# A causal convolution over eight taps: half of one more output pair moved from VectorE to ScalarE and GpSimd, later output buffers, tap 0 in four parts, and new instruction orders

## The chip, the cores and the metric

The kernel runs on one core of one Trainium2 chip. The time is the device time of one execution in microseconds. A core has TensorE (PE, the matrix engine; its weight loads are shown apart as PEld), VectorE (DVE), ScalarE (ACT), GpSimd (POOL) and SyncE (SP), each with an instruction queue of its own that is worked off in order. Transfers are issued from the queues of SP, POOL and ACT.

## The reference

`x` is (8, 4096, 512) and `kernel` (8, 512, 512), both f32; the output has the form of `x`.

```python
for k in range(K):                      # K = 8 taps
    shifted = x if k == 0 else concatenate([zeros(B, k, D), x[:, :-k, :]], axis=1)
    out += matmul(shifted, kernel[k])
```

Row t of the output is the sum over k of x[t - k] times kernel[k].

## The kernel before

The 8 x 4096 time steps are laid out as 128 partitions of 256 steps each, so that one matmul handles the same step of 128 stretches. The first 4 steps (HEAD) are computed tap by tap (`direct`). The other 252 are 21 blocks of 12 steps. A block is four *nodes*, PL, MI, H1 and H0, numbered k = 1 to 84 (node 4m + 1 is PL of block m). A node makes a part of a convolution out of sums and differences of rows of x and of taps, so that fewer products are needed than in the direct way; two nodes of block 0, k = 3 and 4 (LEAF), go with fewer sums and more products.

A *product* is four matmuls of 128x128 by 128x512 in bf16. A node has 9 of them (a leaf 11), named in the orders below as a1, a0, u, v0, v1, l00, l01, l10, l11. The other steps of a node are:

- DVE: `z` (differences or sums of rows of x, seven rows, XR to Z), `A`, `s` (sums of rows of Z, to S), `F0` and `F1` (sums of rows of S), all bf16 with both inputs in SBUF; `d0` and `d1` (PSUM and the f32 tile DT, to PSUM); `e0` and `e1` (a pair of PSUM banks and an output tile, to an output tile `y`).
- ACT: the copy after a1, the seeds `s0` and `s1` (they start the PSUM pairs of v0 and v1), `dt` (fills DT), the copies of PL's pairs to `cc`, and E0 (the half of an H1 pair).
- POOL: loads of later rows of x (`r0` to `r2`), the halves ga0, gb0, ga1 and gb1 of the middle output rows (cc and dd), and ya0, the second half of H1's first pair.
- SP: the stores and the transposes of x into XR (`x12` to `x20`).

In the order a token is a step and a node counted from the block's PL: `F0.2` is F0 of H1 (0 PL, 1 MI, 2 H1, 3 H0, then 4 PL and 5 MI of the next block), so `z.5` is the z of the next block's MI. DVE works about one node ahead of the products that use its sums. The output tiles come from a pool of five buffers of 128x1024 f32 (`ypool`); a block takes six (cc0, cc1, dd0, dd1, yy0, yy1), so a tile waits for a store of an older one. PSUM has four pairs of banks: pp0 to pp2 are taken in turn by the two pairs of each node, pp3 is the first accumulator of each node.

What sets the order is written by hand: a list of calls for the start, and then the string ORDER, once a block. Within an engine instructions run in just that order. `behind` makes a POOL instruction wait for the latest DVE sum that stands ahead of it in the list.

At the start x and the taps are loaded; tap 0 in one load, the others as loads of 512 KB. Weight sums (`wsum`, `plus`, lines L84 of DVE with 128x2048) prepare the nodes' weights, the first four rows are transposed on PE, and `fill` keeps PE working with matmuls of zeros.

Of the kernel before, what the change touches and what calls it, by code (L numbers as in the profile page):

```python
# [14 lines left out]
def kernel(  # L15
# [244 lines left out]
    def node_e(n, b_):  # L260
        p, t = n.p[b_], n.t + 2 * b_
        first = n.k <= 4
        if n.a == PL:
            cc[b_] = y_tile()
            if first:
                nc.scalar.mul(out=cc[b_], in_=p, mul=0.5)
            else:
# [2 lines left out]
                nc.scalar.mul(out=dd[b_], in_=cc[b_], mul=-0.5)  # L270
        elif n.a == MI:
            if first:
                dd[b_] = y_tile()
                stt(dd[b_], p, -0.5, cc[b_], ADD)
            else:
                stt(dd[b_], p, 0.5, dd[b_], ADD)
        elif n.a == H1:
            yy[b_] = yy.get(b_) or y_tile()
            if first or b_ == HI:
                tt(yy[b_], p, dd[b_], ADD if first else SUB)  # L280
                store(t, yy.pop(b_))
            else:
                tt(yy[b_][:, 0], p[:, 0], dd[b_][:, 0], SUB)
        elif n.k == len(nodes) - 1 and b_ == HI:
            for j, eng in ((HI, nc.scalar), (LO, nc.sync)):
                stt(dd[b_][:, j], dd[b_][:, j], -1.0, p[:, j], SUB)
                eng.dma_start(out=orr[:, t + 8 + j, :], in_=dd[b_][:, j])
        else:
            if first:
                tt(dd[b_], dd[b_], p, SUB)  # L290
            else:
                stt(dd[b_], dd[b_], -1.0, p, SUB)
# [2 lines left out]
    def node_E(n):
        if n.a == H1 and n.k > 4:
            yy[LO] = yy.get(LO) or y_tile()
            nc.scalar.copy(out=yy[LO][:, 1], in_=n.p[LO][:, 1])

    def node_y(n):  # L300
        if n.a == H1 and n.k > 4:
            y = yy.pop(LO)
            behind(nc.gpsimd.tensor_tensor(out=y[:, 1], in0=y[:, 1], in1=dd[LO][:, 1], op=SUB))
            store(n.t, y)
# [4 lines left out]

    def middle_half(n, b_, j):  # L310
        behind(nc.gpsimd.tensor_tensor(out=cc[b_][:, j], in0=cc[b_][:, j], in1=dd[b_][:, j], op=ADD), b_ > j and n.k)  # L311
# [143 lines left out]
    fill(pair(3))
    fill(pair(3))
    here(nc.scalar.copy, 0, "x0", 0, 2)
    transpose_pe("h4", 3, H, 4, 8)
    here(nc.scalar.copy, 0, "x0", 2, 4)
    fill(pair(2))  # L460
    history(nc.scalar.copy, -4, "h4")
    direct(0, 1)
    go(3, "v0")
    go(2, "d1")
    direct(0, 0)
    direct(0, 2)
    direct(0, 3)
    direct(4, 2)
    fill(pair(2))
    load_w(1)  # L470
    direct(4, 0)
    direct(1, 1)
    direct(1, 3)
    wsum(MI, HI, HI)
    load_w(5)
    load_w(3)
    wsum(MI, HI, LO)
# [25 lines left out]
    go(4, "F1")
    direct(7, 3)
    wsum(MI, LO, LO)
    history(nc.scalar.copy, -7, "h3")
    direct(6, 3)
    wsum(H0, MID, HI)
    plus((LO, HI))
    direct(3, 2)  # L510
    direct(6, 2)
    direct(5, 2)
    direct(5, 0)
    direct(2, 1)
    wsum(MI, LO, HI)
    transpose_pe("x4", 3, xin[4], 0, 4)
    wsum(PL, MID, HI)
    transpose_pe("x8", 2, xin[8], 0, 2)
    direct(7, 0)
    here(nc.scalar.copy, 4, "x4", 0, 2)  # L520
    wsum(MI, LO, MID)
    wsum(PL, LO, MID)
    wsum(MI, MID, HI)
# [179 lines left out]
```

## Time and profile before

| | us |
|---|---|
| three runs | 717.39, 718.18, 718.66 (median 718.18) |
| span of the profiled execution, first to last instruction | 717.2 |
| PE busy | 696.0 (97%) |
| DVE busy | 683.3 (95%) |
| ACT busy | 287.7 (40%) |
| POOL busy | 167.5 (23%) |

The profile is one execution; the page gives its span, and no other time of its own. The three runs are whole executions, and their median stands 1.0 us above the span. The page groups instructions by line, engine and tile. "Idle before" is the engine's time without work ahead of them, and the releaser is what ended it. The timeline lists one engine's instructions in order with start and duration; the chain of waits follows what ended last backwards; the windows give each engine's busy time within a stretch.

### The profile page before, as it was taken

The numbers are of one execution on the slowest core, as the hardware profiler recorded it, in microseconds if no ns is written. First come the engines' busy times: TensorE is split into PE (matmuls) and PEld (weight loads), VectorE is DVE, ScalarE is ACT, GpSimd is POOL, SyncE is SP. The second block draws the span as 40 slices with busy tenths as digits, with TensorE's granted clock in tenths as the row PEclk, the third lists the DMA queues.
The fourth block names the chain that finished last, engine by engine and source line by source line (L and its number), as shares of the span: only waits on it lengthen the run. The fifth ranks groups of instructions, "written<-read, shape, count | busy, mean of one in ns | idle before, by whom it ended". The sixth has DMA issues, their size and how long they took to land.

```text
span 717.2 us, 8960 instructions
## 1 busy us (share of the span) xinstructions
PE 696.0 (97%) x3205; PEld 315.0 (44%) x3270; DVE 683.3 (95%) x767; ACT 287.7 (40%) x448; POOL 167.5 (23%) x180
## 2 busy tenths in 40 slices
PE   7989999999999999999999999999999999999995
PEld 3444444444444444444444444444444444444442
DVE  1899999999999999999999999999999999999994
ACT  3043244343435444343443434353443434444341
POOL 4200012213131221304122131312213041221212
PEclk9999999999999999999999999999999999999999
DMA  9996988788797878879788887977788698855414
GB/s 194 209 225 139 235 156 243 158 233 181 206 226 174 233 167 231 181 189 217 182 241 158 231 184 205 229 176 229 168 237 174 189 224 178 238 119 186 157 68 175
DMA packets 159515, 138.86 MB, mean 194 GB/s; under 512 B 130160, under 2 KB 134256, under 8 KB 159344
## 3 DMA queue, kind: packets, MB, share of 16 engines
q1 hardware_dynamic: 145312, 99.37, 46.6%
q0 software_dynamic: 13728, 38.15, 31.6%
q10 hardware_dynamic: 432, 0.79, 0.3%
q8 instruction: 25, 0.41, 0.2%
q14 instruction: 18, 0.15, 0.1%
HBM read 77.33 MB, written 99.09 MB: 246 GB/s over the span
## 4 chain that ended last, share of the span: by engine, by line
PE 84%; DVE 5%; issue 5%; DMA 0%; POOL 0%; DVEq 0%; POOLq 0%
PE pp L127 84%; DVE w L84 2%; DVE Z L84 2%; DVE y L87 1%; DVE S L84 1%; DMA out_dram<-y 0%; POOL y L311 0%; DVE y L84 0%; DVE F L84 0%; DVE pp L87 0%; DVE pp L84 0%; POOL xd L93 0%; DVEq L84 0%; DVEq L87 0%; POOLq L93 0%
## 5 line engine op out<-in xcount | busy, mean ns | idle before, releaser
L127 PE MATMUL pp<-w,F 128*128 128x512 bf16 x1285 | 310.4, 379 | 3.2 <-DVE pp L87 1.3
L127 PE MATMUL pp<-w,Z 128*128 128x512 bf16 x941 | 231.9, 379 | 2.7 <-DVE Z L84 1.7
L127 PEld LDWEIGHTS <-F 128*128 128x128 bf16 x1312 | 128.3, 98 | 157.6 <-issue 3.4
L311 POOL TENSOR_TENSOR y<-y 128x512 f32<-128x512 f32 x80 | 101.7, 1272 | 406.0 <-DVE F L84 266.1
L127 PE MATMUL pp<-w,S 128*128 128x512 bf16 x658 | 157.5, 379 | 0.7
L84 DVE TENSOR_TENSOR Z<-XR 128x2048 bf16<-128x2048 bf16 (+3 forms) x109 | 154.5, 1435 | 2.5
L127 PEld LDWEIGHTS <-Z 128*128 128x128 bf16 x960 | 92.3, 98 | 118.2 <-DVE Z L84 9.4
L198 ACT COPY pp<-pp 128x512 f32<-128x512 f32 x82 | 46.7, 570 | 221.1 <-PE pp L127 221.1
L84 DVE TENSOR_TENSOR S<-Z 128x2560 bf16<-128x2560 bf16 (+1 forms) x81 | 114.5, 1413 | 0.0
L84 DVE TENSOR_TENSOR F<-S 128x1024 bf16<-128x1024 bf16 x160 | 111.1, 694 | 1.9 <-PE pp L127 1.9
L127 PEld LDWEIGHTS <-S 128*128 128x128 bf16 x672 | 65.8, 98 | 79.4 <-issue 0.2
L214 ACT COPY pp<-pp 128x512 f32<-128x512 f32 (+1 forms) x84 | 48.9, 582 | 76.5 <-PE pp L127 76.5
L93 POOL DMA_DIRECT2D xd<-in_x_dram x61 | 32.7, 536 | 103.7 <-DVE F L84 48.6
L84 DVE TENSOR_TENSOR pp<-DT,pp 128x512 f32<-128x512 f32 x82 | 56.3, 687 | 0.2 <-PE pp L127 0.2
L87 DVE SCALAR_TENSOR_TENSOR pp<-pp,DT 128x512 f32<-128x512 f32 x82 | 56.5, 689 | 0.0
L216 ACT ACTIVATE pp<-pp 128x512 f32<-128x512 f32 (+1 forms) x84 | 50.1, 596 | 15.2 <-PE pp L127 9.8
L84 DVE TENSOR_TENSOR Z<-Z 128x1024 bf16<-128x1024 bf16 x78 | 53.4, 684 | 0.7
L87 DVE SCALAR_TENSOR_TENSOR y<-pp,y 128x1024 f32<-128x1024 f32 x42 | 51.0, 1215 | 0.0
L220 ACT COPY DT<-pp 128x512 f32<-128x512 f32 x82 | 48.9, 597 | 2.6 <-PE pp L127 2.6
L268 ACT COPY y<-pp 128x1024 f32<-128x1024 f32 x40 | 40.6, 1016 | 22.9 <-PE pp L127 21.7
L87 DVE SCALAR_TENSOR_TENSOR y<-y,pp 128x1024 f32<-128x1024 f32 (+1 forms) x41 | 48.3, 1181 | 0.3 <-PE pp L127 0.3
L270 ACT ACTIVATE y<-y 128x1024 f32<-128x1024 f32 x40 | 42.3, 1057 | 2.8 <-DMA out_dram<-y 0.6
(35 smaller groups left out, 248.5 us busy)
## 6 DMA issues: line engine op xcount, KB each, us to landing
out_dram<-y SPq DMA_DIRECT2D x126, 512.0 KB, 4.2
xd<-in_x_dram POOLq DMA_DIRECT2D x61, 512.0 KB, 5.6
w<-in_kernel_dram POOLq DMA_DIRECT2D x8, 512.0 KB, 16.8
w<-in_x_dram SPq DMA_DIRECT2D x1, 1024.0 KB, 4.8
w<-in_x_dram POOLq DMA_DIRECT2D x2, 512.0 KB, 14.0
XR<-xd SPq DMA_TRANSPOSE x61, 4.8
out_dram<-y ACTq DMA_DIRECT2D x3, 256.0 KB, 3.4
w<-in_x_dram POOLq DMA_DIRECT2D x2, 256.0 KB, 18.1
```

The costliest lines, as they stand in the source:

```text
L84: last["dve"] = nc.vector.tensor_tensor(out=o, in0=a, in1=b, op=op)
L87: last["dve"] = nc.vector.scalar_tensor_tensor(out=o, in0=a, scalar=by, in1=b, op0=MUL, op1=op)
L93: return nc.gpsimd.dma_start(out=o, in_=src)
L127: nc.tensor.matmul(bank, lhsT=comp[:, c * P:(c + 1) * P], rhs=w[:, c, :], start=start and c == 0, stop=c == DC - 1, skip_group_check=True)
L198: nc.scalar.copy(out=n.q[:, 0], in_=n.q[:, 1])
L214: nc.scalar.copy(out=o, in_=q)
L216: nc.scalar.mul(out=o, in_=q, mul=-1.0)
L220: nc.scalar.copy(out=DT, in_=n.q[:, 0])
L268: nc.scalar.copy(out=cc[b_], in_=p)
L270: nc.scalar.mul(out=dd[b_], in_=cc[b_], mul=-0.5)
L311: behind(nc.gpsimd.tensor_tensor(out=cc[b_][:, j], in0=cc[b_][:, j], in1=dd[b_][:, j], op=ADD), b_ > j and n.k)
```

## The change

**H1's second pair.** `SPLIT = (0, 1)`: for both pairs of H1 DVE now adds only the first half. The other half is copied by ACT (E1) and completed by POOL (ya1).

**Output buffers and algebra.** `cc` is written as 0.5 p (before: p) and doubled by ACT later (m0, m1) instead of a -0.5 copy to `dd`; `dd` is now made by DVE at MI, one node later, in a fresh buffer. H0's last operation becomes a plain subtraction. In block 0 the middle rows are made by POOL in halves, not by DVE (g0, g1).

**S of H1 and F.** H1's `s` is written with its five rows in reverse, H0's at rows 1 to 4; F sums adjacent rows then, without the repeated or strided operands of before.

**The start.** Tap 0 is loaded as four transfers and multiplied in four column parts, 22 early filler matmuls instead of 14, the cast of the first rows is split otherwise, a copy goes to DVE, and the order of sums, loads and transposes is new.

**The orders.** ORDER and the list at the start (SETUP) are new throughout.

```diff
-LEAF, EARLY = (3, 4), 6
+LEAF, EARLY, SPLIT = (3, 4), 6, (0, 1)
...
+            self.rev = a == H1 and not self.leaf
...
         if n.shares:
-            tt(n.s[:, 0:4], n.z[:, n.o + 1:n.o + 5], n.z[:, n.o + 3:n.o + 7], ADD)
...
+            tt(n.s[:, 1:5], z[:, o + 1:o + 5], z[:, o + 3:o + 7], ADD)
+        elif n.rev:
+            tt(n.s[:, ::-1], z[:, o:o + 5], z[:, o + 2:o + 7], ADD)
...
+        i = 2 - a if n.rev and not n.whole else a
+        tt(F[:, a:b], n.s[:, i:i + b - a], n.s[:, i + 1:i + 1 + b - a], ADD)
...
         if n.a == PL:
             cc[b_] = y_tile()
-            if first:
-                nc.scalar.mul(out=cc[b_], in_=p, mul=0.5)
-            else:
-                nc.scalar.copy(out=cc[b_], in_=p)
-                dd[b_] = y_tile()
-                nc.scalar.mul(out=dd[b_], in_=cc[b_], mul=-0.5)
+            nc.scalar.mul(out=cc[b_], in_=p, mul=0.5)
         elif n.a == MI:
-            if first:
-                dd[b_] = y_tile()
-                stt(dd[b_], p, -0.5, cc[b_], ADD)
-            else:
-                stt(dd[b_], p, 0.5, dd[b_], ADD)
+            dd[b_] = y_tile()
+            stt(dd[b_], p, -0.5, cc[b_], ADD)
         elif n.a == H1:
             yy[b_] = yy.get(b_) or y_tile()
-            if first or b_ == HI:
-                tt(yy[b_], p, dd[b_], ADD if first else SUB)
+            if b_ in SPLIT:
+                tt(yy[b_][:, 0], p[:, 0], dd[b_][:, 0], ADD)
+            else:
+                tt(yy[b_], p, dd[b_], ADD)
                 store(t, yy.pop(b_))
...
+    def node_E(n, b_):
+        yy[b_] = yy.get(b_) or y_tile()
+        nc.scalar.copy(out=yy[b_][:, 1], in_=n.p[b_][:, 1])
+
+    def node_y(n, b_):
+        y = yy.pop(b_)
+        behind(nc.gpsimd.tensor_tensor(out=y[:, 1], in0=y[:, 1], in1=dd[b_][:, 1], op=ADD))
+        store(n.t + 2 * b_, y)
+
+    def twice(n, b_):
+        nc.scalar.mul(out=cc[b_], in_=cc[b_], mul=2.0)
...
+    def direct_part(c):
+        w = W[(K - 1) >> 2, (K - 1) >> 1 & 1, (K - 1) & 1]
+        for t in range(HEAD):
+            nc.tensor.matmul(pd[t // 2][:, t % 2], lhsT=XR[:, place(t), c * P:(c + 1) * P], rhs=w[:, c, :],
+                             start=c == 0, stop=c == DC - 1, skip_group_check=True)
...
     ORDER = """
...
-        d1.3 e0.3 u.4 l11.3 z.5 s0.4 F0.4 A.5 s1.4 dt.4 ga1.2 v0.4 v1.4 l10.3 d0.4 a1.5 d1.4 l00.4 l01.4
+        E1.2 u.4 dt.4 gb1.2 s0.4 l11.3 l10.3 e0.3 v0.4 z.5 ya1.2 s1.4 F0.4 v1.4 A.5 ga1.2 a1.5 d0.4 d1.4
```

**What moves: DVE and POOL in a block.** DVE around the second half of a block, from H0's d0 to the next PL's d0; `y<-pp,y` is H1's second output pair, `y<-y,pp` H0's first. Before:

```order
L84 TENSOR_TENSOR pp_1348<-DT,pp_1348 128x512
L84 TENSOR_TENSOR y<-pp_1277,y 128x1024
L84 TENSOR_TENSOR S<-Z 128x2560
L87 SCALAR_TENSOR_TENSOR pp_1345<-pp_1345,DT 128x512
L87 SCALAR_TENSOR_TENSOR y<-y,pp_1348 128x1024
L84 TENSOR_TENSOR Z<-XR 128x1536
L84 TENSOR_TENSOR Z<-XR 128x2048
L84 TENSOR_TENSOR F<-S 128x1024
L84 TENSOR_TENSOR Z<-Z 128x1024
L84 TENSOR_TENSOR pp_1400<-DT,pp_1400 128x512
```

Now:

```order
L84 TENSOR_TENSOR pp_1356<-DT,pp_1356 128x512
L87 SCALAR_TENSOR_TENSOR pp_1358<-pp_1358,DT 128x512
L84 TENSOR_TENSOR S<-Z 128x2560
L84 TENSOR_TENSOR y<-pp_1302,y 128x512
L84 TENSOR_TENSOR y<-y,pp_1356 128x1024
L84 TENSOR_TENSOR Z<-XR 128x1536
L84 TENSOR_TENSOR Z<-XR 128x2048
L84 TENSOR_TENSOR F<-S 128x1024
L84 TENSOR_TENSOR Z<-Z 128x1024
L84 TENSOR_TENSOR pp_1414<-DT,pp_1414 128x512
```

H1's second add shrinks to 128x512 and stands behind d1 of H0 and S of the next PL. POOL in the same block, with the buffers' numbers and what each row waits for. Before (L303 is ya0, L311 the middle halves):

```order
L311 TENSOR_TENSOR y_1205<-y_1205,y_1207 128x512 [waits DVE_49]
L93 DMA xd_1338<-in_x_dram 128x2048 [waits DMASW6_49,DVE_49]
L303 TENSOR_TENSOR y_1328<-y_1328,y_1207 128x512 [waits DMAHW4_49,DVE_49,DMAHW6_49,Activation_49,Pool_49]
L93 DMA xd_1360<-in_x_dram 128x2048 [waits DMASW7_49]
L311 TENSOR_TENSOR y_1270<-y_1270,y_1272 128x512 [waits DMAHW4_49,DMAHW0_49,DVE_49]
L311 TENSOR_TENSOR y_1270<-y_1270,y_1272 128x512 [waits DVE_49]
```

Now (L293 is ya0 and ya1, L300 the middle halves):

```order
L300 TENSOR_TENSOR y_1227<-y_1227,y_1279 128x512 [waits DVE_49]
L93 DMA xd_1373<-in_x_dram 128x2048 [waits DMASW1_49,DVE_49]
L293 TENSOR_TENSOR y_1348<-y_1348,y_1279 128x512 [waits DMAHW6_49,DMAHW4_49,Activation_49]
L93 DMA xd_1395<-in_x_dram 128x2048 [waits DMASW2_49,DVE_49]
L300 TENSOR_TENSOR y_1268<-y_1268,y_1330 128x512 [waits DMAHW3_49,DVE_49,Activation_49]
L293 TENSOR_TENSOR y_1405<-y_1405,y_1330 128x512 [waits DMAHW2_49,DVE_49,Activation_49]
L300 TENSOR_TENSOR y_1268<-y_1268,y_1330 128x512 [waits DVE_49]
```

The new add ya1 (y_1405) stands between the two middle halves gb1 and ga1, behind DVE's z of the next block's MI.

**ACT ahead of H0's seeds.** From the copy after H0's a1 to its dt. Before (L298 is E0, L216 and L214 the seeds):

```order
L198 COPY pp_1298<-pp_1298 128x512
L298 COPY y<-pp_1274 128x512
L216 ACTIVATE pp_1345<-pp_1298 128x512
L214 COPY pp_1348<-pp_1298 128x512
L220 COPY DT<-pp_1298 128x512
```

Now (L289 is E0, L297 m1, L218 and L220 the seeds, L224 dt):

```order
L202 COPY pp_1318<-pp_1318 128x512
L289 COPY y<-pp_1304 128x512
L297 ACTIVATE y<-y 128x1024
L218 COPY pp_1356<-pp_1318 128x512
L220 ACTIVATE pp_1358<-pp_1318 128x512
L224 COPY DT<-pp_1318 128x512
```

The doubling of cc1 stands between E0 and the first seed, and the two seeds change places.

**DVE at the start, up to the first node's A.** Weight tiles have numbers (w_71 is tap 7's); w_97 holds the first node's A and S. Before:

```order
L84 TENSOR_TENSOR w_96<-w_96 128x2048
L84 TENSOR_TENSOR w_89<-w_87,w_88 128x2048
L84 TENSOR_TENSOR w_96<-w_96 128x2048
L84 TENSOR_TENSOR w_94<-w_91,w_88 128x2048
L84 TENSOR_TENSOR w_96<-w_96 128x2048
L84 TENSOR_TENSOR Z<-XR 128x2560
L84 TENSOR_TENSOR w_97<-Z 128x1024
L84 TENSOR_TENSOR w_97<-Z 128x1536
L84 TENSOR_TENSOR Z<-XR 128x1024
L84 TENSOR_TENSOR w_78<-w_75,w_72 128x2048
```

Now:

```order
L84 TENSOR_TENSOR w_85<-w_83,w_81 128x2048
L84 TENSOR_TENSOR w_96<-w_96 128x2048 x2
L84 TENSOR_TENSOR Z<-XR 128x2560
L84 TENSOR_TENSOR Z<-XR 128x1024
L84 TENSOR_TENSOR w_97<-Z 128x1024
L84 TENSOR_TENSOR w_97<-Z 128x1536
L84 TENSOR_TENSOR w_97<-Z 128x1024
L84 TENSOR_TENSOR w_93<-w_90,w_87 128x2048
```

Of the rows before, the sums w_89, w_94 and w_93 come behind the first node's A and S, w_78 ahead of its z; the second part of z (128x1024) comes ahead of A.

More of the change, by code (lines that the diff above doesn't have):

```diff
@@ L287, in node_e @@
                 eng.dma_start(out=orr[:, t + 8 + j, :], in_=dd[b_][:, j])
         else:
[L289 to L292, printed above, removed]
+            tt(dd[b_], dd[b_], p, SUB)
             store(t + 8, dd[b_])
[L295 to L304, printed above, removed]
@@ L306, in middle @@
-    def middle(n, b_):
-        stt(cc[b_], cc[b_], 2.0, dd[b_], SUB)
-        store(n.t + 4 + 2 * b_, cc[b_])
+    def node_E(n, b_):
[7 more added lines that the diff above has]
+        nc.scalar.mul(out=cc[b_], in_=cc[b_], mul=2.0)
     def middle_half(n, b_, j):
-        behind(nc.gpsimd.tensor_tensor(out=cc[b_][:, j], in0=cc[b_][:, j], in1=dd[b_][:, j], op=ADD), b_ > j and n.k)
+        behind(nc.gpsimd.tensor_tensor(out=cc[b_][:, j], in0=cc[b_][:, j], in1=dd[b_][:, j], op=SUB), b_ > j and n.k)
@@ L455 @@
[L455 to L477, printed above, removed]
@@ L503 @@
[L503 to L523, printed above, removed]
@@ new lines, with act @@
+    """.split()
+    def act(token):
+        name, _, k = token.partition(".")
+        if token in FIRST:
+            FIRST[token]()
+        elif k:
+            if name in PARTS:
+                done.add((name[0], int(k)))
+                PARTS[name](nodes[int(k)])
+            else:
+                do(name, int(k))
+        elif name.startswith("out"):
+            direct_out(int(name[3:]))
+        elif name[0] == "f":
+            fill(pair(int(name[1:])))
+        elif name[0] == "w":
+            load_w(int(name[1:]))
+        elif name[0] == "T":
+            transpose_x(int(name[1:]))
+        elif name[0] == "L":
+            load_x(int(name[1:]))
+        elif name[0] == "B":
+            behind(load_x(int(name[1:])))
+        elif name[0] == "t":
+            p = PE_T[name[1:]]
+            transpose_pe(name[1:], *p)
+        elif name[0] == "q":
+            n, c = K - 1, int(name[1:])
+            load(W[n >> 2, n >> 1 & 1, n & 1][:, c:c + 1], kr[:, c:c + 1, 0, :])
+        elif name[0] == "P":
+            direct_part(int(name[1:]))
+        elif name[0] in "cv":
+            t, h = int(name[2:3]), name[3:]
+            lo = 0 if h == "a" else 2
+            src = "x" + str(t)
+            here(nc.scalar.copy if name[0] == "c" else nc.vector.tensor_copy, {0: 0, 4: 4, 8: 8, 9: 10}[t], src, lo, lo + 2)
+        elif name[0] == "D":
+            direct(int(name[1]), int(name[2]))
+        elif name[0] in "sp":
+            a, b_, c_ = (int(i) for i in name[1:])
+            if name[0] == "p":
+                plus((b_, c_))
+            else:
+                wsum(a, b_, c_)
```

254 lines of the change are left out of this document (55 added, 199 removed).

## The prediction

> **What bounds the kernel now.** I read the page first, then the waits, the chain of waits, the middle of the run by windows and by groups, and last the timelines of VectorE (DVE), GpSimd (POOL) and TensorE (PE) at the start, in one block and at the end. The page, and under it the middle by windows (columns: us, then busy us of PE, weight loads, DVE, ACT, POOL, clock, DMA):
>
> ```profile
> PE 696.0 (97%) x3205; PEld 315.0 (44%) x3270; DVE 683.3 (95%) x767; ACT 287.7 (40%) x448; POOL 167.5 (23%) x180
> PE pp L127 84%; DVE w L84 2%; DVE Z L84 2%; DVE y L87 1%; DVE S L84 1%; DMA out_dram<-y 0%; POOL y L311 0%; DVE y L84 0%; DVE F L84 0%; DVE pp L87 0%; DVE pp L84 0%; POOL xd L93 0%; DVEq L84 0%; DVEq L87 0%; POOLq L93 0%
> ...
> 310.00:550.00 240.00, 238.84 (x1090) 107.98 (x1110) 238.02 (x273) 102.32 (x164) 59.70 (x61) 1.00 0.81 200
> ```
>
> PE carries 84% of the chain, but in the middle DVE is busy 238.02 of 240.00 us: both are full, at clock 1.00. The chain gives PE's pace and shows the one place in the middle where it leaves PE:
>
> ```profile
> 282.52 10.74 PE pp L127 x49
> 293.26 0.05 issue
> 293.32 7.52 PE pp L127 x34
> ...
> 303.11 1.21 DVE y L87
> ...
> 307.52 9.02 PE pp L127 x41
> ```
>
> A piece repeats every 10.74 + 0.05 = 10.79 us. It lists 49 matmuls, but 1110 weight loads in 240.00 us make 0.216 us each, so 50 matmuls stand in 10.79 (one record is missing): 0.2158 us per matmul. A block has 4 nodes of 36, 144 matmuls = 31.08 us. The DVE timeline (start, us) shows one block of the same engine from Z to Z:
>
> ```profile
> 319.47 1.21 DVE L84 TENSOR_TENSOR Z<-XR 128x2048 bf16<-128x2048 bf16 x1
> ...
> 332.27 1.48 DVE L84 TENSOR_TENSOR S<-Z 128x2560 bf16<-128x2560 bf16 x1
> 333.67 0.69 DVE L87 SCALAR_TENSOR_TENSOR pp<-pp,DT 128x512 f32<-128x512 f32 x1
> 334.27 1.21 DVE L87 SCALAR_TENSOR_TENSOR y<-y,pp 128x1024 f32<-128x1024 f32 x1
> 335.40 2.08 DVE L84 TENSOR_TENSOR Z<-XR 128x1536 bf16<-128x1536 bf16 x2
> 337.40 0.68 DVE L84 TENSOR_TENSOR F<-S 128x1024 bf16<-128x1024 bf16 x1
> 338.00 0.68 DVE L84 TENSOR_TENSOR Z<-Z 128x1024 bf16<-128x1024 bf16 x1
> 338.61 0.68 DVE L84 TENSOR_TENSOR pp<-DT,pp 128x512 f32<-128x512 f32 x1
> ...
> 339.81 0.78 DVE L84 TENSOR_TENSOR F<-S 128x1024 bf16<-128x1024 bf16 x1
> ...
> 350.70 1.22 DVE L84 TENSOR_TENSOR Z<-XR 128x2048 bf16<-128x2048 bf16 x1
> ```
>
> 350.70 - 319.47 = 31.23: DVE needs 0.15 us a block more than PE, so by a hair DVE sets the pace and PE waits for it. The waits agree (us in total, times, longest):
>
> ```profile
> PEld L127 <- DVE Z L84: 9.4, 20, 1.2
> DVE y L84 <- DMA out_dram<-y: 3.0, 2, 1.6
> ```
>
> The 20 waits of weight loads on Z are one a block, mostly hidden, since a load runs ahead of its matmul. The other row is two waits of DVE for a store that still reads an output buffer; one is the chain's gap at 300.83.
>
> **Start and end.** DVE, then PE, then the last rows:
>
> ```profile
> 25.79 1.23 DVE L84 TENSOR_TENSOR w<-w,w 128x2048 bf16<-128x2048 bf16 x1 [1.21 <-DMA w<-in_kernel_dram]
> ...
> 40.88 1.21 DVE L84 TENSOR_TENSOR w<-w 128x2048 bf16<-128x2048 bf16 x1
> 42.02 1.48 DVE L84 TENSOR_TENSOR Z<-XR 128x2560 bf16<-128x2560 bf16 x1
> 43.53 1.56 DVE L84 TENSOR_TENSOR w<-Z 128x1024 bf16<-128x1024 bf16 x2
> 45.01 0.68 DVE L84 TENSOR_TENSOR Z<-XR 128x1024 bf16<-128x1024 bf16 x1
> 45.62 1.22 DVE L84 TENSOR_TENSOR w<-w,w 128x2048 bf16<-128x2048 bf16 x1
> ```
>
> ```profile
> 12.27 4.48 PE L127 MATMUL pp<-w,XR 128*128 128x512 bf16 x20 [1.50 <-DMA w<-in_kernel_dram]
> ...
> 44.28 1.04 PE L127 MATMUL pp<-w,w 128*128 128x512 bf16 x4 [2.10 <-DVE w L84]
> 45.16 1.03 PE L127 MATMUL pp<-w,XR 128*128 128x512 bf16 x4
> 46.02 0.59 PE L351 MATMUL pp<-DT 128*128 128x512 bf16 x2
> ```
>
> ```profile
> 706.24 3.62 PE L127 MATMUL pp<-w,F 128*128 128x512 bf16 x15
> ...
> 707.40 2.51 POOL L311 TENSOR_TENSOR y<-y 128x512 f32<-128x512 f32 x2 [0.65 <-DVE y L84]
> ...
> 710.31 1.19 ACTq L287 DMA_DIRECT2D out_dram<-y  x1
> ```
>
> From the landing of tap 7 (25.79) to the first node's z (42.02) DVE makes 14 weight sums, 1.14 apart (40.88 to 42.02). PE waits 2.10 for that node's A and begins a1 at 44.28. Its last matmul ends at 709.86; the span is 717.2, so 7.3 us follow. From 44.28 to 709.86, 665.6 us, PE runs 82 x 36 = 2952 matmuls of nodes, 88 of leaves, 12 direct and 2 fillers: 3054 x 0.2158 = 659.1. So PE loses 6.5: by the waits up to 3.0 at the two stores, the rest in the first blocks and at Z.
>
> **The change, part by part.**
>
> *H1's second pair.* One DVE add of 1024 becomes one of 512; ACT copies the other half (E1) and POOL adds to it (ya1). The middle by groups:
>
> ```profile
> L84 DVE TENSOR_TENSOR y<-pp,y 128x1024 f32<-128x1024 f32 x7 | 8.5, 1215 | 0.0
> L84 DVE TENSOR_TENSOR y<-pp,y 128x512 f32<-128x512 f32 x8 | 5.4, 678 | 0.0
> L298 ACT COPY y<-pp 128x512 f32<-128x512 f32 x8 | 4.7, 586 | 15.4 <-DVE y L84 15.4
> L303 POOL TENSOR_TENSOR y<-y 128x512 f32<-128x512 f32 x8 | 10.2, 1271 | 5.0 <-issue 5.0
> ```
>
> DVE's add shrinks from 1215 to 678 ns, 0.54 a block: 31.23 becomes 30.69, below PE's 31.08, with 0.39 to spare. The end of the middle is then set by PE. E1 (586 ns) goes to an ACT that is busy 102.32 of 240.00, ya1 (1271 ns) to a POOL at 59.70 of 240.00: neither engine is full, so their time costs nothing by itself. Their place in the queues can: E1 frees a PSUM pair, ya1 stands ahead of the middle half ga1 on POOL and of its store on SP, and behind E0 and m1 ACT now issues the seed that PE's v0 of H0 needs. I cost this at nothing while PE still has earlier products to run there, and keep the rest for the rivals. What is late next if this cover goes is v0 of H0.
>
> *The half difference.* ACT still makes one operation from PSUM and one from SBUF for each half pair (0.5 and 2.0 in place of a copy and -0.5); DVE's adds keep form and size. That is nothing on either engine. The output buffer of dd is now taken at MI, and H1's second add stands behind d1 of H0 and s of the next PL: by the rows at 332.27 and 333.67 these are steps of 1.40 and 0.60, so 2.0 us later. The store that it waits for starts no later than before. The longest store wait was 1.6, so both go: -2.8 (PE had some cover, so a little less than 3.0); nothing at worst, if another buffer takes over the wait.
>
> *Setup.* Of the 14 weight sums between tap 7 and z 12 are left: two go into DVE's waits for taps (one is the 1.21 at 25.79), two behind z, and two others come ahead of it. 2 x 1.14 = 2.28. The last two rows of z now stand ahead of A, + 0.61 (45.01 to 45.62). A begins 1.67 earlier and a1 at 42.6 instead of 44.28. One product with tap 6 and one filler, which PE ran after a1 (45.16 and 46.02), now come before it, into the wait. Bounds: no gain, if loads or POOL hold the start where it was, and 2.9, if PE also gets the 1.2 of those two; I take the arithmetic of a1, 1.7, and count the rest through the number of matmuls.
>
> *Tap 0, casts, fillers.* PE waits 1.50 for tap 0, and later 2.10 at a1 for DVE. Whatever the four parts and eight more early fillers do lies ahead of that second wait, which covers it: nothing. Without the cover the parts are worth at most the 1.50; the four loads in place of one cost three more issues on POOL ahead of the taps, below the 0.54 each that an xd load shows:
>
> ```profile
> 323.94 0.54 POOL L93 DMA_DIRECT2D xd<-in_x_dram  x1
> ```
>
> Loads of later rows of x change places on POOL's queue (rows 40 and 32 go before rows 12 to 28): two issues, 1.1 us, for rows that blocks 0 and 1 transpose much later. Nothing; a wait for XR early in the run would show it.
>
> *S of H1 written in reverse, F in new places.* Same elements and types, so I take the same time; a slow reversed write is a rival.
>
> *Block 0 of the output.* Two 1.2 us DVE operations on the middle pair go to POOL in four halves. The chain leaves DVE for PE by 53 us, so this is hidden: nothing.
>
> *End.* After the last products POOL has three adds in place of the two at 707.40 (2.51 for both): 1.27 more. The last outputs leave at 710.3, and the span ends at 717.2, so some of it is covered by transfers that are still draining: + 0.7, between 0 and 1.6.
>
> **Sum.** PE from a1: 42.6 + 3052 matmuls x 0.2158 (658.6) = 701.2. Of the loss of 6.5, the stores' 2.8 go, and of the other 3.7 I keep 2.0: the part at Z goes with DVE's spare, the first blocks stay tight (bounds 0.5 and 3.7). PE ends at 703.2. Add 7.3 + 0.7: a span of 711.2. The median of the runs, 718.18, stands 1.0 above the profiled span of 717.2, so 712.2, some 6 us faster. With all bounds together this case reaches from 709 to 716.
>
> **Rivals.**
>
> *POOL's new add holds DVE up (slower).* Row for row:
>
> ```profile
> 338.76 1.27 POOL L311 TENSOR_TENSOR y<-y 128x512 f32<-128x512 f32 x1 [3.66 <-DVE Z L84]
> ```
>
> This add runs until 340.03, and the F that starts at 339.81 beside its end takes 0.78 instead of 0.68: 0.22 of overlap cost 0.10. Now POOL's adds start beside DVE operations that read PSUM (d at 338.61 here). The new ya1 is released by the z of the next MI (335.40) instead, with F of PL (337.40) and A of MI (338.00) next, both with two inputs in SBUF. If ya1 gets in after F, A waits for 1.27 - 0.12 = 1.15. If DVE's next operation keeps ya1 out until d, it costs 0.10 as now. 1.15 less the spare of 0.39 is 0.76 a block, x 20 = 15: 727. It decides from 0.39 a block on, and is slower overall from 0.39 + 6/20 = 0.7. For it: nothing but F's and A's inputs; against it: the POOL adds shown all take 1.27, so none was held, and DVE's operations follow each other without a gap.
>
> The Trainium skill, "SBUF — State Buffer", section "Who interferes with whom", has a rule that speaks against this change: a DVE instruction with two SBUF inputs shares a read interface with a GpSimd instruction that reads SBUF, and who issues first keeps it for the whole instruction. F's 0.10 agrees in kind. By the rule the result is 727 if POOL issues first between F and A, and 712 if DVE does; no run so far shows which.
>
> *ACT is late for v0 of H0 (slower).* m1 (like L270, 1057 ns) and E0 (586) now precede the seed. If PE lacks cover by 0.5 us a block, 10 us in all: 722. Against it: ACT is 43% busy.
>
> ```profile
> L270 ACT ACTIVATE y<-y 128x1024 f32<-128x1024 f32 x16 | 16.9, 1057 | 0.9
> ```
>
> *The reversed S runs at the rate of f32.* From 678 to 1215 ns are 512 elements, 1.05 ns each; 2560 such elements are 2.8 instead of 1.48: + 1.3 a block, 0.9 over the spare, 18 us: 730. No row has a reversed operand.
>
> *Little arrives (same).* The start is held by loads, the losses at Z stay, the end costs its full 1.6: 718.2 - 2.8 + 1.6 = 717.
>
> **Chances.** A measurement tells about 0.2% (1.4 us) from no change. Forecast 0.58, with small holds still faster 0.04; little arrives 0.09; POOL's hold 0.21, ACT 0.05, reversed S 0.03. So faster 0.62, same 0.09, slower 0.29. The likeliest is 712.2; its own range is 709 to 716, and with POOL's hold the range is 709.5 to 727.
>
> **What the profile after would show.** Right: DVE busy about 31.08 - 0.4 per 31.08 us and waiting for PE; no wait of DVE or ACT for a store in the middle; the chain on PE in pieces of 10.79 from about 43 on; a1 at 42.6; H1's S at 1.48; the A of MI at 0.68. Wrong: A or F at 1.5 to 1.9 and a chain that goes through Z every block; PE waiting for ACT at v0 of H0; a block above 31.2; POOL's last add more than 2 us behind the last matmul.

## The result and the profile after

The changed kernel takes 750.34 us (median of six runs, 740.26 to 755.52), the kernel before on the same chip 718.22 us: slower by 32 us where 6 us faster was forecast. The ratio of 1.036 [1.033, 1.040], some 26 us, leaves out the three slow runs of the six, those over 1.5% above the fastest, and counts 740.26, 743.80 and 748.04. The changed kernel's runs also lie 15 us apart, those of before 2. The profiled execution, with a span of 738.3 us, belongs to its fastest run.

The page of the changed kernel, the busy times and then the chain's shares by line, the middle by windows (columns as before), and three of its waits (us in total, times, longest):

```profile
PE 698.2 (95%) x3209; PEld 314.8 (43%) x3274; DVE 705.1 (96%) x766; ACT 296.8 (40%) x471; POOL 213.7 (29%) x209
PE pp L127 58%; DVE Z L84 17%; DVE S L84 4%; DVE y L84 4%; DVE F L84 3%; DVE pp L87 2%; DVE pp L84 2%; PE pp L340 1%; DMA xd<-in_x_dram 1%; DMA XR<-xd 1%; PE pp L346 0%; PE pp L379 0%; SPq L100 0%; DVE w L84 0%; ACT XR L358 0%
```

```profile
310.00:550.00 240.00, 230.27 (x1046) 103.30 (x1066) 238.52 (x263) 99.51 (x163) 70.41 (x66) 1.00 0.81 197
```

```profile
PEld L127 <- DVE Z L84: 37.5, 40, 3.7
PE pp L127 <- DVE Z L84: 22.7, 20, 3.2
...
DVE Z L84 <- DMA XR<-xd: 2.4, 2, 2.0
```

DVE has half an add less to do in each block and yet is busy 705.1 us instead of 683.3. The chain, 84% PE before, is 58% PE and 17% Z of DVE. PE's waits on Z rose from 9.4 us to 37.5 for the weight loads, and from 1.7 to 22.7 for the matmuls (these are the same stretches seen twice, not a sum). No wait of DVE for a store is left; a wait for XR, transposed rows of x, is new. The clock is 1.00: PE isn't slow, it is kept waiting.

DVE and then POOL in one block (start, us). The row at 312.28 is F of PL, the one at 312.88 A of MI, and the last the A of the block after; 301.62 and 324.00 are a z and an S with no add beside them. POOL's adds are ya0, gb1, ya1 and ga1 in this order:

```profile
301.62 2.02 DVE L84 TENSOR_TENSOR Z<-XR 128x3584 bf16<-128x3584 bf16 x1
...
306.57 1.77 DVE L84 TENSOR_TENSOR S<-Z 128x2560 bf16<-128x2560 bf16 x1
...
309.99 2.37 DVE L84 TENSOR_TENSOR Z<-XR 128x3584 bf16<-128x3584 bf16 x1
312.28 0.68 DVE L84 TENSOR_TENSOR F<-S 128x1024 bf16<-128x1024 bf16 x1
312.88 1.75 DVE L84 TENSOR_TENSOR Z<-Z 128x1024 bf16<-128x1024 bf16 x1
...
324.00 1.48 DVE L84 TENSOR_TENSOR S<-Z 128x2560 bf16<-128x2560 bf16 x1
...
345.30 1.75 DVE L84 TENSOR_TENSOR Z<-Z 128x1024 bf16<-128x1024 bf16 x1
```

```profile
305.70 1.28 POOL L293 TENSOR_TENSOR y<-y 128x512 f32<-128x512 f32 x1
308.64 0.54 POOL L93 DMA_DIRECT2D xd<-in_x_dram  x1 [1.66 <-DVE S L84]
309.19 1.28 POOL L300 TENSOR_TENSOR y<-y 128x512 f32<-128x512 f32 x1
312.49 1.59 POOL L293 TENSOR_TENSOR y<-y 128x512 f32<-128x512 f32 x1 [2.02 <-ACT pp L220]
314.72 1.27 POOL L300 TENSOR_TENSOR y<-y 128x512 f32<-128x512 f32 x1 [0.63 <-DVE Z L84]
```

A takes 1.75 instead of 0.68, and ends (314.63) 0.55 after ya1 (314.08): ya1 went ahead when F ended, and A's own work followed behind it. S at 306.57 and z at 309.99, beside ya0 and gb1, take 1.77 and 2.37 where 1.48 and 2.02 are the undisturbed times. That is 1.07 + 0.29 + 0.35 = 1.71 a block lost for 0.54 saved: 1.17 more, and the block went from 31.23 to 32.42 by these two rows of A (345.30 - 312.88), to 32.33 over the five from 215.94 to 377.57. Where the add was first, the price is the time side by side less 0.12 or 0.13: 0.41 cost S 0.29, 0.48 cost z 0.35, 1.20 cost A 1.07. DVE's instructions with an input in PSUM pay nothing: between 200 and 600 us 115 of them run beside such an add for more than 0.1 us, and none takes over 0.02 more than alone.

The start: the first node's A on DVE, a1 on PE, POOL's loads of x, SP's transposes, and weight loads (second number of the windows) in a stretch behind it, of before and of after:

```profile
41.68 2.16 DVE L84 TENSOR_TENSOR w<-Z 128x1024 bf16<-128x1024 bf16 x3
```

```profile
42.67 1.03 PE L127 MATMUL pp<-w,w 128*128 128x512 bf16 x4
```

```profile
30.79 2.59 POOL L93 DMA_DIRECT2D xd<-in_x_dram  x5 [11.38 <-DVE w L84]
47.81 1.02 POOL L93 DMA_DIRECT2D xd<-in_x_dram  x2 [14.43 <-DVE F L84]
55.02 1.02 POOL L93 DMA_DIRECT2D xd<-in_x_dram  x2 [6.19 <-DVE w L84]
```

```profile
52.68 14.43 SPq L100 DMA_TRANSPOSE XR<-xd  x3
```

```profile
75.00:106.00 31.00, 30.81 (x142) 13.94 (x144) 30.89 (x34) 12.38 (x19) 2.90 (x5) 1.00 0.92 197
```

```profile
75.00:106.00 31.00, 26.76 (x122) 11.93 (x123) 28.79 (x30) 11.44 (x18) 9.51 (x9) 1.00 0.82 180
```

a1 begins at 42.67, 1.6 earlier. But then 123 weight loads stand where 144 stood: 21 x 0.216 = 4.5 us lost between 75 and 106. The chain there passes through "DMA xd<-in_x_dram" and "DMA XR<-xd", and DVE waits 2.0 us for XR.

The end, PE, DVE and POOL:

```profile
725.30 3.61 PE L127 MATMUL pp<-w,F 128*128 128x512 bf16 x16 [0.21 <-DVE pp L84]
```

```profile
729.94 0.69 DVE L84 TENSOR_TENSOR y<-y,pp 128x512 f32<-128x512 f32 x1 [1.43 <-POOL y L293]
731.17 0.69 DVE L84 TENSOR_TENSOR y<-y,pp 128x512 f32<-128x512 f32 x1 [0.54 <-POOL y L300]
```

PE ends at 728.91; 9.4 us follow, 7.3 before. DVE's last halves overwrite the output tile that POOL's ya1 and ga1 still read.

So the profiled run: from a1 to PE's last matmul are 686.2 us, of which 3052 x 0.2158 = 658.6 are work. 27.6 are lost where the forecast had 2.0: 4.5 between 75 and 106, and from 137 on, about 18.3 blocks, 32.33 - 31.08 = 1.25 each, 22.9. The tail is 1.4 longer than forecast. 25.6 + 1.4 and 0.1 at a1 are the 27.1 between 711.2 and 738.3. The median of the runs lies 10 to 12 us above that; no profile shows what a run in that place loses, and the experiments on loads bear on it.

### The profile page after: what moved, and what is told of

It is laid out like the page before. It is cut to its first block, busy times and chain, and to the rows that moved or that the text cites. A ratio compares the mean times of both kernels' runs of the same rounds, so it can differ in the third digit from the quotient of the medians.

```text
span 738.3 us, 9068 instructions
## 1 busy us (share of the span) xinstructions
PE 698.2 (95%) x3209; PEld 314.8 (43%) x3274; DVE 705.1 (96%) x766; ACT 296.8 (40%) x471; POOL 213.7 (29%) x209
## 4 chain that ended last, share of the span: by engine, by line
PE 61%; DVE 32%; issue 4%; DMA 2%; ACT 1%; SPq 0%; POOL 0%; POOLq 0%; DVEq 0%
PE pp L127 58%; DVE Z L84 17%; DVE S L84 4%; DVE y L84 4%; DVE F L84 3%; DVE pp L87 2%; DVE pp L84 2%; PE pp L340 1%; DMA xd<-in_x_dram 1%; DMA XR<-xd 1%; PE pp L346 0%; PE pp L379 0%; SPq L100 0%; DVE w L84 0%; ACT XR L358 0%
## 5 line engine op out<-in xcount | busy, mean ns | idle before, releaser
L127 PE MATMUL pp<-w,Z 128*128 128x512 bf16 x942 | 231.9, 379 | 23.6 <-DVE Z L84 22.7
L84 DVE TENSOR_TENSOR Z<-XR 128x2048 bf16<-128x2048 bf16 (+3 forms) x109 | 161.5, 1500 | 5.4 <-DMA XR<-xd 2.4
L300 POOL TENSOR_TENSOR y<-y 128x512 f32<-128x512 f32 x84 | 108.0, 1286 | 152.3 <-DVE F L84 78.8
L127 PEld LDWEIGHTS <-Z 128*128 128x128 bf16 x960 | 91.4, 98 | 141.8 <-DVE Z L84 37.5
L84 DVE TENSOR_TENSOR S<-Z 128x2560 bf16<-128x2560 bf16 (+1 forms) x81 | 120.4, 1486 | 0.0
L293 POOL TENSOR_TENSOR y<-y 128x512 f32<-128x512 f32 x42 | 61.7, 1469 | 59.1 <-ACT pp L220 40.5
L84 DVE TENSOR_TENSOR Z<-Z 128x1024 bf16<-128x1024 bf16 x78 | 73.6, 943 | 0.0
L220 ACT ACTIVATE pp<-pp 128x512 f32<-128x512 f32 (+1 forms) x84 | 49.4, 589 | 52.0 <-PE pp L127 49.6
L224 ACT COPY DT<-pp 128x512 f32<-128x512 f32 x82 | 49.2, 600 | 18.5 <-PE pp L127 18.5
L289 ACT COPY y<-pp 128x512 f32<-128x512 f32 x42 | 24.6, 585 | 72.8 <-DVE y L84 72.8
L218 ACT COPY pp<-pp 128x512 f32<-128x512 f32 (+1 forms) x84 | 49.5, 590 | 9.9 <-PE pp L127 8.0
L84 DVE TENSOR_TENSOR y<-y,pp 128x1024 f32<-128x1024 f32 (+1 forms) x43 | 50.9, 1183 | 2.6 <-POOL y L293 1.4
L268 ACT ACTIVATE y<-pp 128x1024 f32<-128x1024 f32 x42 | 43.1, 1027 | 24.3 <-PE pp L127 23.1
```

Source lines behind the costliest of these rows:

```text
L84: last["dve"] = nc.vector.tensor_tensor(out=o, in0=a, in1=b, op=op)
L127: nc.tensor.matmul(bank, lhsT=comp[:, c * P:(c + 1) * P], rhs=w[:, c, :], start=start and c == 0, stop=c == DC - 1, skip_group_check=True)
L218: nc.scalar.copy(out=o, in_=q)
L220: nc.scalar.mul(out=o, in_=q, mul=-1.0)
L224: nc.scalar.copy(out=DT, in_=n.q[:, 0])
L289: nc.scalar.copy(out=yy[b_][:, 1], in_=n.p[b_][:, 1])
```

## The experiments

Two suspects: POOL's adds beside DVE's sums in every block, and the x loads at the start. All times are medians; the ratio is to the kernel before on the same chip. A block's time is read from the weight loads between 200 and 600 us: 400 x 144 / their count (after: 1785, 32.27; before 1835, 31.39 with its two waits for stores).

### POOL's adds

**A memset in the place of ya1.** It leaves H1's second half without its last sum from node 5 on, and writes zeros there.

```diff
-        behind(nc.gpsimd.tensor_tensor(out=y[:, 1], in0=y[:, 1], in1=dd[b_][:, 1], op=ADD))
+        behind(nc.gpsimd.memset(y[:, 1], 0.0))      # b_ == HI and n.k > 4
```

> The changed kernel, with POOL's new add ya1 replaced from block 1 on by a fill of the same half tile with zeros, which reads nothing (so the second half of H1's second pair is left out of the output). Theory 'port' (DVE's A, two SBUF inputs, is held by a POOL add that reads SBUF): A of MI back from 1.75 to about 0.68 us, a block 32.27 - 1.07 = 31.2, span about 719 to 721. Rival 'any POOL work' or 'something else holds A' (ACT's new copy, the buffers): A stays at 1.7, span about 738.

733.75 us, 1.019 [1.015, 1.023]; the block 31.27 (1842 loads).

```profile
L84 DVE TENSOR_TENSOR Z<-Z 128x1024 bf16<-128x1024 bf16 x78 | 53.2, 682 | 0.0
L294 POOL MEMSET y<- 128x512 f32 x20 | 10.5, 525 | 39.3 <-ACT pp L220 38.7 <-issue 0.6
```

The mean A fell from 943 to 682 ns with the same releaser, place and tile, so it is not E1 or the buffers that hold A. The memset starts 0.19 us after F and takes 0.52 to 0.53 beside it, and F keeps its 0.68; ya1 in that place takes 1.59 instead of 1.28. With the undisturbed PSUM rows this points to what collides: a sum with both inputs in SBUF and an add that reads SBUF. For A itself the run says less, since the memset ends as A begins; a fill that lasts through A wasn't tried. A span of 719 to 721 was expected: 1.0 us a block is some 20 us, and by the ratios the time fell by 12. The profiled run, the longest of the four, waits 18.8 us for XR.

**Without the split of H1's second pair** (DVE adds all of it again), everything else as changed.

```diff
-LEAF, EARLY, SPLIT = (3, 4), 6, (0, 1)
+LEAF, EARLY, SPLIT = (3, 4), 6, (0,)
```

> The changed kernel, but H1's second pair added whole by DVE again (no E1, no ya1); all orders as changed. Theory 'port': A 0.68 (-1.07), DVE's add +0.54, a block 31.7, span about 728. Rival 'the split relieves DVE as meant, orders or buffers cost the time': DVE gains 0.54 a block and the span grows to about 748.

735.06 us, 1.020 [1.014, 1.025]; block 31.63 (1821). A is 681 again, but the 38 large z still average 2087 ns and S 1573, where the kernel before has 2024 and 1479.

**ya0 and gb1 moved**, ahead of POOL's load of x and to operations of DVE that read PSUM; ya1 as changed.

```diff
-  dt.3 r1.2 ya0.2 F1.3 d0.3 v1.3 a1.4 d1.3 s.4 l01.3 r2.2 l00.3 a0.4 e1.2 E1.2 u.4 dt.4 gb1.2 s0.4
+  dt.3 F1.3 ya0.2 r1.2 d0.3 v1.3 a1.4 d1.3 s.4 l01.3 gb1.2 r2.2 l00.3 a0.4 e1.2 E1.2 u.4 dt.4 s0.4
```

> The changed kernel with two other POOL adds moved ahead of the loads that stand before them (ya0 behind F1 of H0, gb1 behind S of the next PL), so that they run beside DVE operations on PSUM; ya1 stays. Theory 'port': S back from 1.77 to 1.48, z from 2.37 to 2.08, A still 1.75; a block 32.27 - 0.64 = 31.6, span about 726. Rival 'only A's hold counts, the rest is covered': span within 2 us of 738.

735.88 us, 1.023 [1.020, 1.026]; block 31.86 (1808). z is 2020 again and A 943 as in the changed kernel; S is 1545 (there 1575), because ya0 now reaches 0.29 us into another S, which takes 1.64. So each stretch belongs to the add beside it, and of the 1.71 two thirds to ya1.

**Both edits.**

> The changed kernel with both: H1's second pair whole on DVE, and ya0 and gb1 moved. Theory 'port': no DVE sum above its undisturbed time by more than 0.1; DVE needs about 31.1 a block, as much as PE; span about 715 to 718. Rival 'the new order or buffers lose time by themselves': a block stays above 31.5 and the span above 725.

731.34 us (719.12 to 734.42). A 681, z 2020, S 1542, block 31.27 (1842): the blocks are repaired, but 715 to 718 was expected, and the median is 13 us above the kernel before. The profiled run waits 8.8 us for XR.

**The kernel before, with one of its own adds moved to where ya1 stands:** ga1 is released by z of MI instead of by A.

```diff
-        d1.3 e0.3 u.4 l11.3 z.5 s0.4 F0.4 A.5 s1.4 dt.4 ga1.2 v0.4 v1.4 l10.3 d0.4 a1.5 d1.4 l00.4 l01.4
+        d1.3 e0.3 u.4 l11.3 z.5 ga1.2 s0.4 F0.4 A.5 s1.4 dt.4 v0.4 v1.4 l10.3 d0.4 a1.5 d1.4 l00.4 l01.4
```

> The kernel before, with one word of its order moved: POOL's add ga1 is released by z of the next MI instead of by A, so that F of PL and A of MI come next on DVE, as ya1 in the changed kernel. Theory 'port': A of MI 0.68 to about 1.75 in nearly every block, a block 31.23 + 1.0 = 32.2, the span 717 + 20 = 737. Rival 'the hold needs the changed kernel's buffers or ACT's work': A stays at 0.68 and the time at 718.

721.42 us, 1.005 [1.003, 1.006]: a miss, if in the right direction. One block of it, DVE (F, A, d) and POOL:

```profile
338.31 0.68 DVE L84 TENSOR_TENSOR F<-S 128x1024 bf16<-128x1024 bf16 x1
338.91 0.68 DVE L84 TENSOR_TENSOR Z<-Z 128x1024 bf16<-128x1024 bf16 x1
339.51 0.69 DVE L84 TENSOR_TENSOR pp<-DT,pp 128x512 f32<-128x512 f32 x1
```

```profile
338.47 2.25 POOL L311 TENSOR_TENSOR y<-y 128x512 f32<-128x512 f32 x1 [2.46 <-DVE Z L84]
```

Here the add is the one that waits: 2.25 us instead of 1.27, kept out through F and A until d, in 15 of 19 blocks; in 4 A took 1.75, and 4 x 1.07 = 4.3 is about the 3.3 us lost. It starts 0.154 to 0.162 us after F. In the changed kernel ya1 starts 0.21 after F (312.49 to 312.28) and gets in ahead of A in all 19. So 0.05 us goes with another outcome, but the start alone doesn't decide: the 4 starts that got in ahead of A (0.154, 0.155, 0.160, 0.162) lie among those that didn't. What decides stays open. E1, for which ya1 also waits, had ended 2.9 us before.

**ya1 released by F0 of PL, ya0 and gb1 moved, loads as before** (the loads are the subject below).

```diff
-  ... z.5 ya1.2 s1.4 F0.4 v1.4 A.5 ga1.2
+  ... z.5 s1.4 F0.4 ya1.2 v1.4 A.5 ga1.2
```

> e9_after_loads with ya0 and gb1 moved beside PSUM work, and ya1 released by F of the next PL, one step later, so that A is already running; split kept. Theory 'no free place': A back to 0.68, but ya1 now takes the place of ga1 beside d, ga1 comes later and DVE's e1 of H0, which overwrites what ga1 reads, waits about 1 us for POOL: a block 31.5, 722 to 726. Rival 'one step is enough': no wait for POOL, block 31.1, 712 to 715.

726.74 us, 1.012 [1.011, 1.014]; block 31.72 (1816).

```profile
306.44 0.68 DVE L84 TENSOR_TENSOR Z<-Z 128x1024 bf16<-128x1024 bf16 x1
...
308.37 1.65 DVE L84 TENSOR_TENSOR F<-S 128x1024 bf16<-128x1024 bf16 x1
```

```profile
306.65 1.60 POOL L293 TENSOR_TENSOR y<-y 128x512 f32<-128x512 f32 x1 [2.50 <-ACT pp L220]
308.21 1.26 POOL L300 TENSOR_TENSOR y<-y 128x512 f32<-128x512 f32 x1
```

The time is in the expected 722 to 726 but for 0.7, by another way than expected: no wait of DVE's e1 of H0 for POOL in the blocks. A is free, but ga1 directly behind ya1 now holds F1 of PL. In the places tried, the hold moves from one sum to the next.

### The loads of x

**Rows 16 loaded one place earlier in the changed kernel**, ahead of a load that waits.

```diff
-  ... D71 L12 s121 ...        ... out1 l00.1 L16 e0.1 ...
+  ... D71 L12 L16 s121 ...    ... out1 l00.1 e0.1 ...
```

> The changed kernel with one load moved on POOL's queue: rows 16 to 19 of x right behind rows 12, ahead of the load that waits for F0 of the first node. Theory 'load order' (this load sits behind a waiting one and comes about 20 us late, and the wait for it is what spreads the times of the changed kernel's runs, lower clock included): no wait of DVE for XR near 62 us, all runs within 5 us, median about 737 instead of 750. Rival 'the spread is the chip's, not the kernel's': runs still spread over 10 us or more, median about 750.

742.68 us (742.55 to 743.87), 1.034 [1.033, 1.036]. The runs now agree to 1.3 us, but the ratio is hardly under 1.036; a wait for XR of 3.6 remains, and most of the loss.

**The kernel before with rows 16, 32 and 36 behind a waiting load of rows 48.**

```diff
+    behind(load_x(48))
+    load_x(16)
+    load_x(32)
+    load_x(36)
```

> The kernel before with the same fault in its loads: rows 48 are loaded behind F0 of the first node, and rows 16 behind that on POOL's queue. Theory 'load order': DVE waits for XR near 60 to 65 us, by some us to some tens, runs spread over 5 us or more and lie at 720 to 740. Rival: the load still lands in time, 718 with a spread under 2.5 us.

722.39 us, 1.005 [1.004, 1.007], with 3.8 us of waits for XR. The four loads leave POOL together at 51.94, behind a wait of 21.82 for F: a load that waits passes its wait on to those behind it on POOL's queue, and here that costs some 4 us. Whether rows 16 are late or four loads beside the transposes slow them, this run doesn't separate. The spread stays at 1.2 us, where 5 or more was expected.

**The changed kernel with the load order of before:** rows 12 to 36 in order and unheld, rows 40, 48 and 52 behind block 0's transposes, and rows 24 transposed ahead of block 0's stores.

```diff
-  D50 B40 L32 ... L12 ... L20 ... L28 ... F0.1 r0.7 ... L16 ... B48 F0.2 ... L24 T12 ... T20 ... L36 ... T24
+  L12 L16 L20 L24 L28 L32 L36 ... F0.1 ... F0.2 ... T12 ... T20 T24 ... z.5 B48 ... A.6 B40 B44 ... a0.7 r0.7
```

> The changed kernel with the loads of x on POOL's queue as in the kernel before: rows 12 to 36 in order of use, none of them behind a waiting load, rows 40 and on only after the first transposes; rows 24 are transposed ahead of block 0's stores. Blocks unchanged. Theory 'loads in flight beside the transposes of the start cost the wait for XR and the spread': transposes at 50 to 66 us land in about 5 us instead of 10 to 30, DVE waits under 1 us for XR, runs spread under 3 us; what is left is the blocks: 18 x 1.04 + tail 2, less the start's 2 and the stores' 3: about 734. Rival 'the spread has another cause': runs still spread over 8 us, median above 740.

736.90 us (736.68 to 737.71), 1.027 [1.026, 1.028], no wait for XR, block 32.31 (1783). So the loads cost some 7 us by the ratios (1.036 to 1.027), 13.4 by the medians of all runs, and with them goes all but 1 us of the spread. In the profiled run 139 weight loads stand between 75 and 106 us: 16 x 0.216 = 3.5 of the 4.5 lost there came from the loads; the rest is about one hold of A (1.07).

**Both repairs to the adds, loads in order, but rows 52, 48 and 40 early** (against the changed kernel, beside SPLIT and the moved adds):

```diff
-  D50 B40 L32 ... L12 ... L20 ... L28 ... F0.1 r0.7 ... L16 ... B48 F0.2 ... L24 T12 ... T20 ... L36 ... T24
+  L12 L16 ... L20 ... L24 L28 L32 L36 ... F0.1 r0.7 ... B48 B40 F0.2 ... T12 ... T20 T24
```

> e4_both (pair whole on DVE, ya0 and gb1 moved) with the loads of x in the order of their use ahead of the first waiting one, and the transposes of rows 24 ahead of the stores of block 0. Theory 'port and load order are the whole loss': start 2 us ahead of the kernel before, no wait for XR, a block about 31.1, no wait for a store: 712 to 715, faster than the kernel before. Rival 'another part of the change also costs time': 718 or more.

735.71 us, 1.024 [1.018, 1.029]; DVE waits 22.9 us for XR, once; 712 to 715 was expected. **With those three late too,** which is all the load order of before (rows 20 to 36 also go a little earlier, 56 and 60 later; the last experiment shows that this isn't what counts):

```diff
-  F0.1 r0.7 ... B48 B40 F0.2 ...
+  F0.1 ... F0.2 ... z.5 B48 ... A.6 B40 B44 ... a0.7 r0.7
```

> The same loads with H1's second pair whole on DVE and ya0 and gb1 beside PSUM work (e4_both and e9_after_loads together). Theory 'port holds and loads are the whole loss': no wait for XR, no wait for a store, a block 31.1, a1 near 42: 712 to 714, faster than the kernel before by 4 to 6. Rival 'something else in the change costs time too': 717 or more.

715.59 us (12 runs, 714.89 to 717.79), 0.998 [0.997, 0.999]: faster than the kernel before by 2.3 us.

```profile
PE 697.3 (98%) x3209; PEld 314.7 (44%) x3274; DVE 685.9 (96%) x766; ACT 284.7 (40%) x450; POOL 178.3 (25%) x188
PE pp L127 78%; DVE Z L84 6%; DVE y L84 2%; DVE S L84 2%; DVE F L84 1%; PE pp L340 1%; DVE pp L84 1%; DVE pp L87 1%; PE pp L346 0%; PE pp L379 0%; DVE w L84 0%; DVE y L87 0%; ACT XR L358 0%; ACT XR L362 0%; DVE DT L439 0%
```

The chain is mostly PE's again. This version has the early a1, the later output buffers and POOL's middle rows in block 0; it does without ya1. DVE still sets its pace, at 31.32 a block (1839), and it gains 2.3 us where 4 to 6 was expected.

**Which early load it is.** First the kernel before with two early loads, rows 48 and 40; then the 715.6 version with one (rows 52), two (rows 48, 40) and all three; then the kernel before with three (rows 52 are then left out of its block loop).

```diff
+    behind(load_x(52))      # three only
+    behind(load_x(48))
+    behind(load_x(40))
...
-    behind(load_x(48))
-    behind(load_x(40))
...
-  F0.1 ... F0.2 ... z.5 B48 ... A.6 B40 B44 ... a0.7 r0.7
+  F0.1 r0.7 ... F0.2 ... z.5 B48 ... A.6 B40 B44 ... a0.7         one
+  F0.1 ... B48 B40 F0.2 ... z.5 ... A.6 B44 ... a0.7 r0.7         two
+  F0.1 r0.7 ... B48 B40 F0.2 ... z.5 ... A.6 B44 ... a0.7         three
```

> The kernel before with two loads (rows 48 and 40, which nothing needs before 100 us) issued about 20 and 30 us earlier, so that they are in flight when rows 12, 16 and 20 are transposed; every load that the transposes need keeps its place. Theory 'collision': the transposes land in 7 us or more, DVE waits for XR, 720 or more. Rival 'only late rows matter, not the neighbours': 718, no wait for XR.

718.14 us, 1.000 [0.9995, 1.0013]: no cost, where 720 or more was expected from the collision.

> The kernel of 715.6 us with only the load of rows 52 moved, from block 0's loop to the start, two nodes earlier than rows 48 and 40 stand in the other kernel of this call. If the count in flight decides, one load does nothing: 715 to 717. If this load, the first to be in flight, pushes the transposes and all later loads back: 720 or more, with a wait of DVE for XR. I lean to 716.

716.12 us.

> The kernel of 715.6 us with two of its later loads, rows 48 and 40, issued ahead of block 0's transposes instead of behind them, nothing else. If such loads slow the transposes by being in flight beside them, whatever else is early: 5 to 20 us slower (720 to 736), a wait of DVE for XR of 5 us or more, transposes that land after 15 us or more. If two loads are few enough, as they were in the kernel before (718.1, landing up to 11.3): 715 to 717 and no such wait; then the third load, rows 52, or the late place of the others made the 735.7. I lean to 716.

715.22 us.

> The kernel of 715.6 us with all three loads early, rows 52 a node ahead of rows 48 and 40. One early load gave 716.1 and two 715.2, both as none. If three in flight at once are what makes the transposes late: 725 to 737, transposes that land after 20 us or more, DVE waiting 10 us or more for XR. If the other moves in the kernel of 735.7 us did it (its later loads in another order): 715 to 718. I lean to 732.

734.11 us, 1.021 [1.018, 1.024].

> The kernel before with three loads early, rows 52, 48 and 40, where two early ones had cost nothing (718.1). If the count in flight decides, the third makes transposes land after 15 us or more, DVE waits for XR some us, and the time is 721 to 735. If the kernel before is safe because its transposes are needed later or its loads stand in order: 718 to 719. I lean to 724.

720.38 us, 1.003 [1.002, 1.004], where two gave 718.1; it waits 2.5 us for XR.

Block 0's transposes and the stretch of 60 to 75 us (PE, weight loads, DVE, ACT, POOL, clock, DMA share, GB/s), first with two early loads, then with three and with the wait of DVE that it makes:

```profile
52.17 16.84 SPq L100 DMA_TRANSPOSE XR<-xd  x4
```

```profile
60.00:75.00 15.00, 15.00 (x72) 6.79 (x70) 14.97 (x14) 7.02 (x8) 5.57 (x3) 1.00 0.99 181
```

```profile
52.32 37.61 SPq L100 DMA_TRANSPOSE XR<-xd  x4
```

```profile
60.00:75.00 15.00, 4.92 (x23) 2.05 (x21) 1.83 (x3) 2.88 (x3) 0.00 (x0) 0.73 1.21 55
75.00:100.00 25.00, 12.17 (x50) 5.24 (x51) 13.87 (x12) 4.17 (x6) 4.74 (x3) 0.68 0.91 122
```

```profile
85.42 1.23 DVE L84 TENSOR_TENSOR Z<-XR 128x2048 bf16<-128x2048 bf16 x1 [23.58 <-DMA XR<-xd]
```

With the third load in flight beside them the four transposes occupy SP's queue for 37.61 us instead of 16.84, the DMA engines' busy share reads 1.21 while they move 55 GB/s instead of 181 (at a share of 0.99), and the granted clock reads 0.73 and 0.68 in the two stretches that hold the gap. Two loads hide, three don't: in this version it is a step, not a price per load. The count alone doesn't give the price, though. The kernel before loses only 2.5 us with the same three, and the changed kernel has four loads there, rows 52, 16, 48 and 24, and waits 2.4 us for XR in its profiled run. In both the transposes go in two groups, three and one; whether that spares them, or a later need of the rows, wasn't tried, and why the engines move so little is open.

## Why the prediction was wrong, point by point

- **"H1's second pair", cost "at nothing".** The step that failed first. Between the changed kernel and the 715.6 version lie 34.7 us by the medians of all runs; 21.3 of them (736.9 - 715.6, both with before's loads) are POOL's adds, 2.5 of these at the end. The hold was known: the rival "POOL's new add holds DVE up" named F and A, the 1.15 of A (measured 1.07, in every block), the time, 727, and the sign, A at 1.5 to 1.9 (measured 1.75). Its chance, 0.21, rested on "none was held" before. That told of adds beside reads of PSUM, which the new places no longer had. Neither text nor rival priced ya0 and gb1: queued behind loads r1 and r2 they met S (0.29) and z (0.35) of the next nodes, shown by the run that moved them alone.
- **"Loads of later rows of x change places ... Nothing."** The step that had no rival at all: some 7 us by the ratios, 13.4 by the medians. "Two issues, 1.1 us" counted the time to issue. The runs show two other costs: transfers in flight beside the transposes, and loads behind a load that waits. "A wait for XR early in the run would show it" was right.
- **The trigger of the hold.** "If ya1 gets in after F" against "if DVE's next operation keeps ya1 out" was left open, and rightly: both happen, the first in all 19 blocks at a start 0.21 us after F, the second in 15 of 19 at 0.16. The order of instructions can't tell them apart.
- The Trainium skill, "SBUF — State Buffer", section "Who interferes with whom", says that a DVE instruction with two SBUF inputs contends with a GpSimd instruction that reads SBUF, not with one that only writes it. The memset agrees as far as it reaches: beside its 525 ns F keeps 0.68. The PSUM rows agree too: one input in SBUF, and nothing lost beside adds that read it.
- **"End: + 0.7, between 0 and 1.6."** Mis-sized: + 2.1. It counted one more add on POOL, but not that DVE's last two halves overwrite what the adds read (waits of 1.43 and 0.54). In the 715.6 version, without ya1, PE's last matmuls begin at 702.59 and take 3.61, and 6.9 us follow to the end of its span of 713.1.
- **"PE ends ... I keep 2.0" of losses.** Measured 27.6, by the two steps above.
- **Right:** a1 at 42.67 (42.6 said); the two store waits gone; S in reverse 1.48; ACT not late for v0 of H0 (no such row among the waits, nor in the memset version, whose blocks take 31.27 with E1 and m1 in place); tap 0 and the fillers cost nothing that a row shows.
- **Open:** that the spread of the changed kernel's runs comes from waits for XR is inferred from the version with restored loads, whose spread is 1.0. And a version in which POOL's sixth add costs nothing wasn't found: each place tried meets another sum.

## What to carry to other kernels

An engine with spare time is not free: before an add goes to GpSimd, list VectorE's instructions beside its whole duration, and price those that read SBUF twice at the time side by side (here less 0.12 us). Adds that the change only pushes later, behind a load, count as new ones. And cost a moved load by what is in flight beside it and what is queued behind it, not by its issue; here two more transfers cost nothing and the third 18 us.
